# A two-layer-block transformer step on one core: the last mixer's recurrent chain in halves of the output partitions, and its value phase with the operands swapped

## The chip, the core and the metric

The program runs on one NeuronCore of a Trainium2 chip. Five engines matter: TensorE (PE, with its weight loads shown apart as PEld), VectorE (DVE), ScalarE (ACT), GpSimd (POOL) and the sync engine (SP), which issues most transfers. Each works its own queue in order. The metric is the device time of one execution in microseconds (us), lower is better; the figure compared is the median of several runs.

## The reference, cut to what matters

The whole computation is two blocks (`first_block`, `second_block`) over 256 tokens of width 1024. Only two parts of the second block are touched. The first is a gated delta-rule recurrence, run in two directions over 256 context tokens and then 256 tokens of x, with 16 heads of 64 channels:

```python
def wkv_scan(s0, scan_in):
    def step(s, inp):
        w, kk, a, k, v, r = inp
        sa = jnp.einsum('dbhij,dbhj->dbhi', s, kk)
        s = s * w[..., None, :] - sa[..., :, None] * (kk * a)[..., None, :] + v[..., :, None] * k[..., None, :]
        return s, jnp.einsum('dbhij,dbhj->dbhi', s, r)
    return lax.scan(step, s0, scan_in)
```

The second is the last layer of experts: each token has gates on 128 of 16384 experts, and the sum over experts is taken densely, expert row by expert row:

```python
        act = jax.nn.gelu(jnp.einsum('chkd,cd->chk', peer_u[eidx], xc))
        return jnp.einsum('chk,chkd->cd', (gate * act).astype(xc.dtype), peer_v[eidx])
```

## The kernel before

The last mixer is `layer2_mix`. Heads are taken two at a time, so a loop runs over eight pairs i. One round of it holds `chain(i)` (the recurrence of pair i), `inverse(i+1)` (`rw_inverse`, the triangular inverses that the next chain needs), `heads(i+1)` (`diff_head`, softmax attention), `scores(i+2)` (`rw_scores`, which makes the operands of a later chain) and some gate projections. The tile framework's scheduler orders the work of a round on each engine; an engine then runs its list strictly in that order. The last chain, i = 7, stands in `merge`, beside the branch projections (`br`).

`rw_chain` (L1710) cuts the 512 tokens into eight chunks of 64. In each chunk PE works in float32 (two records in the profile for one matmul; a transpose has one) through these steps, every one of which reads the one before:

- `vt` (L1728): two transposes turn 64 values of each direction; ACT copies them into the lower half of `UV` (L1729), whose upper half POOL sets to zero (L1725).
- `R`: state times `AL` (L1734, two matmuls of 128 columns, not in the first chunk), plus `MA` times `UV` over 128 rows, of which 64 are zero (L1738, four matmuls of 64 columns). All land on PSUM partitions 0 to 63. DVE copies the result (L1739).
- `U` (L1744): four matmuls with the inverse `TT`, 64 rows by 64 columns, again all on partitions 0 to 63 (the operands lie in the half that the pair's parity names). ACT negates and copies them into the upper half of `UV` (L1745).
- `Y`, in the last four chunks: `Y` from the state (L1749, two matmuls) and from `UV` (L1753, four matmuls, whose outputs alternate between partitions 0 to 63 and 64 to 127).
- `S` (L1760), in the first seven chunks: two matmuls of 128 columns that give the products of both heads with each other, of which half is then multiplied by the zeros of `WC`. DVE adds the old state (L1767) and multiplies by the decay `WC` (L1768).

`AL` is a copy, made by POOL (L1672), of `self.apart`, a single buffer in which one head stands beside zeros and into which both directions write in turn.

In `peer` the value phase (L2030 on) goes through 128 rows of `v`. A row is split into a high and a low float32r part, as are the gated activations `a`, and `mm` (L415) makes three matmuls of each product (L420 to L422). The row is the stationary operand: eight blocks of 128 columns, with the 256 tokens moving, so 24 matmuls of 256 columns to a row, into four PSUM accumulators laid out as output channels by tokens. Rows 48 to 111 of `a` come back from DRAM by loads on SP's queue (L2025).

## Time and profile before

| | us |
|---|---|
| median of three runs | 3560.41 (3560.06 to 3569.77) |
| the profiled execution | 3562.86 |
| its span in the profile | 3561.1 |
| the mixer's stage, 1520 to 2662 | 1142 |
| of that, the loop over pairs and its setup, to 2560 | 1040 |
| the value phase, first to last of its matmuls | 3139 to 3556 |

Over the span PE is busy 92%, DVE 64%, ACT 48% and POOL 21%. The busy time of PE is a model of pipelined matmuls, so two things are read beside it: when one group of matmuls starts and the next starts, which is the room that it takes in PE's list, and the waits printed behind a group, which name what PE stood still for. The granted clock of a stretch is a share of 2.4 GHz; 0.50 is 1.2 GHz.

### The profile page before, as it was taken

Reading aid. Unit: us, or ns where it says so; the run is one execution under the profiler, and the core shown is the slowest. Engines: PE = TensorE matmul, PEld = TensorE weight load, DVE = VectorE, ACT = ScalarE, POOL = GpSimd, SP = SyncE. Lnnn points to the kernel's source line nnn. Section 1 sums busy time; section 2 is a strip of 40 time slices with the busy share of each in tenths; the row PEclk is TensorE's granted clock in tenths of the full one; section 3 lists DMA queues with packets and bytes.
Section 4 is the critical chain, followed back from the end, with each engine's and each line's share of the span. In section 5 each row is a group of like instructions: output and inputs, shape, how many; then the busy total and the mean of one; then the engine's idle time right before and its main releaser. Section 6 shows DMA issues by size and latency. Waiting matters only on the chain.

```text
span 3561.1 us, 70098 instructions
## 1 busy us (share of the span) xinstructions
PE 3284.8 (92%) x27824; PEld 2789.4 (78%) x27824; DVE 2268.7 (64%) x4481; ACT 1707.5 (48%) x3116; POOL 732.7 (21%) x757
## 2 busy tenths in 40 slices
PE   6989889989999999977889999999889989999999
PEld 4869868866668888645677777767788989999999
DVE  3568847853359999546555655565447767756665
ACT  4445332442236666334334444444436657755554
POOL 0000322200000000013232323233308853300000
PEclk8999987899999999988878998899889999999999
DMA  7666573378788999951101111111336445555665
GB/s 292 243 222 228 208 248 111 122 296 349 320 364 326 341 333 336 379 184 49 32 29 38 52 44 38 35 47 53 115 116 206 163 140 177 174 193 190 232 213 166
DMA packets 164493, 658.65 MB, mean 185 GB/s; under 512 B 18216, under 2 KB 37304, under 8 KB 120256
## 3 DMA queue, kind: packets, MB, share of 16 engines
q1 hardware_dynamic: 149952, 580.72, 45.7%
q0 software_dynamic: 14208, 73.41, 5.7%
q8 instruction: 220, 3.60, 0.4%
q14 instruction: 113, 0.93, 0.1%
HBM read 634.26 MB, written 19.79 MB: 184 GB/s over the span
## 4 chain that ended last, share of the span: by engine, by line
PE 43%; DVE 8%; ACT 3%; issue 1%; DMA 1%; POOL 1%; SPq 0%; DVEq 0%; ACTq 0%; POOLq 0%
PE acc L421 3%; PE acc L420 3%; PE acc L422 3%; PE act L422 3%; PE act L421 3%; PE act L420 3%; PE G L1993 2%; DVE G L1808 1%; PE mc L1688 1%; PE U L1744 1%; PE R L1738 1%; DVE rs L366 1%; PE R L1734 1%; PE S L1760 1%; PE qk L420 1%
## 5 line engine op out<-in xcount | busy, mean ns | idle before, releaser
L1725 POOL MEMSET UV<- 64x256 f32 x64 | 19.4, 304 | 1007.0 <-DVE xT L1174 817.4
L427 PE MATMUL mg<-mg,xs 128*64 128x256 f32 x1408 | 184.9, 386 | 3.7 <-ACT xf L1100 3.7
L1247 ACT ACTIVATE msg<-mg 128x128 f32<-128x128 f32 (+1 forms) x154 | 42.1, 274 | 260.0 <-PE mg L427 190.7
L427 PEld LDWEIGHTS mg<-mg,xs 128*64 128x64 f32 x1408 | 106.1, 138 | 68.2 <-issue 15.8
L330 PE MATMUL mod<-wm,c 128*32 128x256 f32 x1152 | 99.7, 450 | 49.9 <-DMA wm<-mods 45.4
L327 POOL DMA_DIRECT2D wm<-mods x64 | 34.7, 543 | 389.0 <-PE mod L330 362.8
L330 PEld LDWEIGHTS mod<-wm,c 128*32 128x32 f32 x1152 | 37.5, 122 | 87.8 <-DMA wm<-mods 44.7
L1248 DVE TENSOR_TENSOR msg<-msg,mg 128x128 f32<-128x128 f32 (+1 forms) x154 | 43.3, 281 | 76.4 <-ACT msg L1247 75.9
L1983 POOL TENSOR_SCALAR oh<-iota,idx 128x128 f32<-128x128 f32 x44 | 58.3, 1324 | 146.4 <-PE G L1993 146.4
L366 DVE RECIPROCAL rs<-rs 128x256 f32<-128x256 f32 (+1 forms) x24 | 58.0, 2418 | 39.0 <-ACT rs L365 39.0
L1986 ACT ACTIVATE oh<-oh,idx 128x128 f32<-128x128 f32 x212 | 69.1, 393 | 6.9 <-DVE oh L1978 6.9
L1744 PE MATMUL U<-R,TT 64*64 64x64 f32 x512 | 49.4, 242 | 24.2 <-DVE R L1739 20.8
L1744 PEld LDWEIGHTS U<-R,TT 64*64 64x64 f32 x512 | 39.3, 149 | 41.0 <-DVE R L1739 24.2
L1745 ACT ACTIVATE UV<-U 64x256 f32<-64x256 f32 x64 | 24.0, 375 | 96.3 <-PE U L1744 96.1
L1978 DVE TENSOR_TENSOR oh<-iota,idx 128x1024 f32<-128x1024 f32 x53 | 67.6, 1278 | 0.0
L1993 PE MATMUL G<-oh 128*128 128x128 f32 x512 | 62.5, 275 | 0.0
L1151 DVE COPY mgt<-mg 128x128 f32<-128x128 f32 x44 | 12.8, 290 | 74.8 <-PE mg L1144 74.5
L1993 PEld LDWEIGHTS G<-oh 128*128 128x128 f32 x512 | 60.1, 192 | 0.0
L427 PE MATMUL ya<-md,mgt 128*64 128x512 f32 x176 | 55.1, 604 | 4.2 <-DVE mgt L1151 4.1
L1739 DVE COPY R<-R 64x256 f32<-64x256 f32 x64 | 26.5, 414 | 50.9 <-PE R L1738 50.5
L1767 DVE TENSOR_TENSOR S<-S,S 128x256 f32<-128x256 f32 x48 | 20.2, 421 | 56.7 <-PE S L1760 56.5
L1808 DVE TENSOR_TENSOR G<-G,X 128x1 f32<-128x1 f32 (+14 forms) x120 | 53.3, 444 | 3.6
(11876 smaller groups left out, 13541.5 us busy)
## 6 DMA issues: line engine op xcount, KB each, us to landing
mg<-m_gu SPq DMA_DIRECT2D x176, 1024.0 KB, 7.7
md<-m_dn SPq DMA_DIRECT2D x88, 1024.0 KB, 8.0
wm<-mods POOLq DMA_DIRECT2D x64, 1024.0 KB, 6.2
w<-u SPq DMA_DIRECT2D x128, 512.0 KB, 3.4
w<-v SPq DMA_DIRECT2D x128, 512.0 KB, 3.4
w<-w_in SPq DMA_DIRECT2D x132, 256.0 KB, 2.6
w<-e_gu SPq DMA_DIRECT2D x44, 512.0 KB, 4.2
w<-e_in SPq DMA_DIRECT2D x24, 512.0 KB, 4.3
```

The costliest lines, as they stand in the source:

```text
L330: nc.tensor.matmul(ps[32 * j:32 * j + 32, :256], c[:, 2 * kp + k, :], ws[:, 2 * j + k, :], start=kp + k == 0, stop=kp + k == 4)
L366: nc.vector.reciprocal(t[:, :n], t[:, :n])
L420: mm(ps, w.hi, h.hi, start=start, stop=False, **kw)
L421: mm(ps, w.hi, h.lo, start=False, stop=False, **kw)
L422: mm(ps, w.lo, h.hi, start=False, stop=stop, **kw)
L427: mm(ps, w, h, start=start, stop=stop, **kw)
L1744: nc.tensor.matmul(ps[:64, c0_:c0_ + 64], TT[hb, d, o, c], R[hb, d, o], start=True, stop=True)
L1808: v_.tensor_mul(pr[:, :t, :t], G[:, t:t + 1, :t].to_broadcast([128, t, t]), X[:, :t, :t].rearrange("p u s -> p s u"))
L1978: v_.tensor_tensor(o, iota.rearrange("p (a b i) -> p a b i", a=1, b=1).to_broadcast([128, 2, 4, 128]), idx[:, 0:2, 4 * t4:4 * t4 + 4].rear ...
L1983: nc.gpsimd.tensor_scalar(o[:, 0, t], iota, i1, w, op0=OP.is_equal, op1=OP.mult)
L1986: nc.scalar.activation(o[:, 0, t], o[:, 0, t], AF.Copy, scale=w)
L1993: nc.tensor.matmul(ps[:, 128 * t:128 * t + 128], o[:, 1, t], o[:, 0, t], start=True, stop=True)
```

## The change

**In the chain.** The two directions (for R and U) or the two heads (for S and Y) go to the two halves of the output partitions, in alternating matmuls of 64 columns. The state keeps only the products of a head with itself, as [128, 2, 64]; `WC` has no zeros. All values of a pair are turned before the first chunk by four transposes of 128 by 128, and `UV` is one tile for all eight chunks; nothing is set to zero. `MA` times `UV` reads the lower 64 rows alone and stands ahead of the state's part. ACT and DVE share the copy of U. S stands ahead of Y.

**Around it.** `AL` and `self.apart` are one set of four buffers, by parity and direction, so POOL's copies go. `rw_inverse` puts the directions on the two halves of the partitions and shares its copies between ACT and DVE. `lora` has one buffer for two, the gates' tile is shared with the squares of `rw_scores`, `diff_head` turns into a second buffer of `e1`, `merge` has one ring pair and one small tile less.

**In the value phase.** The activations are the stationary operand, in two blocks of 128 tokens, and half a row of `v`, 512 columns, moves: 12 matmuls a row. The spilled activations are loaded on POOL's queue, some rows ahead. At the end the four accumulators, now tokens by channels, are copied to SBUF and turned back by 16 transposes.

```diff
         for a in range(32):
-            nc.tensor.matmul(p2[:32, 16 * a:16 * a + 16], TT[half[0], a, 0:32], P1[half[0], a], start=True, stop=True)
+            d, e = divmod(a, 16)
+            nc.tensor.matmul(p2[32 * d:32 * d + 32, 16 * e:16 * e + 16], TT[half[d][0], e, 0:32], P1[half[d][0], e], start=True, stop=True)
...
+        UV = tp.tile([128, 8, 128], F32, tag="UV", name=f"UV{i}", bufs=UVB)
+        ps = self.psum("vt")
+        for j in range(4):
+            nc.tensor.transpose(ps[:, 128 * j:128 * j + 128], v[:, j // 2, 128 * (j % 2):128 * (j % 2) + 128], self.ident)
+        for h, e in enumerate((nc.scalar.copy, v_.tensor_copy)):
+            e(UV.rearrange("p (j h) x -> p h j x", h=2)[64:128, h], ps[dh[h]].rearrange("p (j x) -> p j x", j=4))
...
-            g_.memset(UV[0:64], 0.0)
...
+            for o in range(2):
+                for d in range(2):
+                    nc.tensor.matmul(ps[dh[d], 64 * o:64 * o + 64], MA[64:128, d, o, c], UV[64:128, js[d], dh[o]], start=o == 0, stop=c == 0 and o == 1, skip_group_check=True)
             if c:
+                for o in range(2):
+                    for d in range(2):
+                        nc.tensor.matmul(ps[dh[d], 64 * o:64 * o + 64], AL[d][:, c, o], S[:, d], start=False, stop=o == 1, skip_group_check=True)
+            v_.tensor_copy(R, ps[:, :128].rearrange("p (o x) -> p o x", o=2))
...
-            nc.scalar.activation(UV[0:64], ps[:64, :256].rearrange("p (d x) -> p d x", d=2), AF.Copy, scale=-1.0)
+            nc.scalar.activation(UV[0:64, js[0]], ps[dh[0], :128], AF.Copy, scale=-1.0)
+            v_.tensor_scalar(UV[0:64, js[1]], ps[dh[1], :128], -1.0, None, op0=OP.mult)
...
+                        nc.tensor.matmul(ps[dh[o], 64 * d:64 * d + 64], BKt[:, d, c, dh[o]], UV[:, js[d], dh[o]], start=True, stop=True)
...
-                    for m in range(KT):
-                        self.mm(acc[m // 2][:, T * (m % 2):T * (m % 2) + T], vs[:, m // 4, 128 * (m % 4):128 * (m % 4) + 128], a[:, j],
-                                i + j == 0 and m % 2 == 0, i + j == 127, skip_group_check=True)
+                    for hf in range(2):
+                        for t in range(2):
+                            self.mm(acc[2 * hf + t], a[:, j, 128 * t:128 * t + 128], vs[:, hf], i + j == 0, i + j == 127)
```

How the lists of the engines move is shown at three places. PE, one late chunk of a chain (the sixth of the last pair), before; R, U, Y, S are the PSUM tiles, the names behind the arrow the operands:

```order
L1734 MATMUL R_26323<-S_4_26313,AL_24886 64x128 x2
L1738 MATMUL R_26323<-UV_5_26316,MA_24887 64x64 x4
L1744 MATMUL U_26331<-R_5_26322,TT 64x64 x4
L1749 MATMUL Y_26337<-AL_24886,S_4_26313 128x64 x2
L1753 MATMUL Y_26337<-MR_24888,UV_5_26316 64x64 x4
L1760 MATMUL S_26345<-UV_5_26316,BKt_24889 128x128 x2
L1728 MATMUL vt_26353<-c_ident,v_25000 64x128 x2
```

And the same chunk in the changed kernel (the part with `AL` alternates twice between its two buffers; one turn is shown):

```order
L1733 MATMUL R_26344<-UV_26200,MA_24908 64x64 x4
L1737 MATMUL R_26344<-S_4_26330,AL_16721 64x64
L1737 MATMUL R_26344<-S_4_26330,AL_16722 64x64
...
L1742 MATMUL U_26354<-R_5_26343,TT_25511 64x64 x4
L1750 MATMUL S_26361<-UV_26200,BKt_24910 64x64 x4
L1763 MATMUL Y_26369<-AL_16721,S_4_26330 64x64 x2
L1763 MATMUL Y_26369<-AL_16722,S_4_26330 64x64 x2
L1766 MATMUL Y_26369<-MR_24909,UV_26200 64x64 x4
```

The transposes are gone from the chunk, the part of R that needs no state stands first, every matmul writes 64 by 64, and S has moved from behind Y to directly behind U.

DVE, a chunk in the middle of the loop (the fifth of a middle pair), before, from the copy of R; G, X are the triangular solve of `rw_inverse`, dst a softmax statistic:

```order
L1739 COPY R_4_21651<-R_21652 64x256
L1639 TENSOR_SCALAR kk_22482<-k_22400,c_pv 128x512
L1511 TENSOR_REDUCE dst_22335<-ds_22341 128x1
L1809 TENSOR_REDUCE X_21861<-G_21794 128x13
L1808 TENSOR_TENSOR G_21794<-G_21794,X_21861 128x14x14
```

And in the changed kernel, from the copy of R to the state's sum:

```order
L1738 COPY R_4_21652<-R_21653 128x128
L1807 TENSOR_REDUCE X_21870<-G_21803 128x14
L1545 SCALAR_TENSOR_TENSOR k_22416<-k_22417,c_pv,k_22416 128x2x255
L1806 TENSOR_TENSOR G_21803<-G_21803,X_21870 128x15x15
L1512 TENSOR_REDUCE dst_22353<-ds_22359 128x1
L1744 TENSOR_SCALAR UV_21545<-U_21663 64x128
L1546 SCALAR_TENSOR_TENSOR k_22416<-k_22417,c_pv,k_22416 128x2x255
L1807 TENSOR_REDUCE X_21870<-G_21803 128x15
L1757 TENSOR_TENSOR S_4_21675<-S_21670,S_3_21649 128x128
```

DVE has got a third step of the chain, the copy of one half of U (L1744 there), with other work queued ahead of it.

PE in the value phase, a piece of one row, before; acc are the accumulators, ap the split activations, w the split row:

```order
L420 MATMUL acc_33671<-ap50h,w28880h 128x256
L421 MATMUL acc_33671<-ap50l,w28880h 128x256
L422 MATMUL acc_33671<-ap50h,w28880l 128x256
L420 MATMUL acc_33672<-ap50h,w28880h 128x256
L421 MATMUL acc_33672<-ap50l,w28880h 128x256
L422 MATMUL acc_33672<-ap50h,w28880l 128x256
```

And in the changed kernel:

```order
L421 MATMUL acc_33699<-w28830h,ap100h 128x512
L421 MATMUL acc_33700<-w28830h,ap100h 128x512
L422 MATMUL acc_33699<-w28830l,ap100h 128x512
L423 MATMUL acc_33699<-w28830h,ap100l 128x512
L422 MATMUL acc_33700<-w28830l,ap100h 128x512
L423 MATMUL acc_33700<-w28830h,ap100l 128x512
```

Each matmul has 512 columns for 256, and there are half as many.

## Rows read from the trace of the kernel before

**Rows 1.** Stretches: us, busy and count of PE, PEld, DVE, ACT, POOL; clock; DMA

```profile
1520.00:2560.00 1040.00, 931.31 (x9406) 727.15 (x9403) 589.64 (x1096) 444.98 (x831) 307.04 (x342) 0.87 0.17 54
3145.00:3550.00 405.00, 405.00 (x3378) 405.00 (x3377) 253.26 (x381) 210.75 (x351) 0.00 (x0) 1.00 0.61 203
```

**Rows 2.** Groups, 1520 to 2662: PE records, busy us, mean ns, idle before

```profile
L1744 PE MATMUL U<-R,TT 64*64 64x64 f32 x512 | 49.4, 242 | 24.2 <-DVE R L1739 20.8 <-DVE TT L1866 3.1
L1738 PE MATMUL R<-UV,MA 128*64 128x64 f32 x512 | 47.7, 243 | 3.5 <-ACT UV L1729 3.5
L1760 PE MATMUL S<-UV,BKt 128*128 128x128 f32 x224 | 44.1, 326 | 6.1 <-ACT UV L1745 6.1
L1734 PE MATMUL R<-S,AL 128*64 128x128 f32 x224 | 41.3, 314 | 12.7 <-DVE S L1768 9.7 <-DVE S L1765 2.8
L1728 PE MATMUL vt<-c_ident,v 128*64 128x128 f32 x128 | 28.2, 304 | 0.7 <-ACT y L1754 0.3
L1749 PE MATMUL Y<-AL,S 128*128 128x64 f32 x128 | 24.4, 320 | 0.0
L1753 PE MATMUL Y<-MR,UV 128*64 128x64 f32 x256 | 17.5, 265 | 1.3 <-ACT UV L1745 1.0
```

**Rows 3.** Timeline, PE, one chunk with nothing beside it: start, us, records, idle before

```profile
2614.09 0.62 PE L1734 MATMUL R<-S,AL 128*64 128x128 f32 x4 [0.85 <-DVE S L1768]
2614.54 0.63 PE L1738 MATMUL R<-UV,MA 128*64 128x64 f32 x8
2615.68 0.67 PE L1744 MATMUL U<-R,TT 64*64 64x64 f32 x8 [0.51 <-DVE R L1739]
2616.29 0.66 PE L1749 MATMUL Y<-AL,S 128*128 128x64 f32 x4
2616.88 0.45 PE L1753 MATMUL Y<-MR,UV 128*64 128x64 f32 x8
2617.26 0.71 PE L1760 MATMUL S<-UV,BKt 128*128 128x128 f32 x4
2617.81 0.38 PE L1728 MATMUL vt<-c_ident,v 128*64 128x128 f32 x2
2619.04 0.51 PE L1734 MATMUL R<-S,AL 128*64 128x128 f32 x3 [0.85 <-DVE S L1768]
```

**Rows 4.** Timeline, PE, two groups of the last chunk, at 1.2 GHz

```profile
2627.33 1.11 PE L1744 MATMUL U<-R,TT 64*64 64x64 f32 x8 [0.51 <-DVE R L1739]
2629.41 0.70 PE L1753 MATMUL Y<-MR,UV 128*64 128x64 f32 x8
```

**Rows 5.** Timeline, DVE and ACT, the chunk of rows 3

```profile
2615.21 0.42 DVE L1739 COPY R<-R 64x256 f32<-64x256 f32 x1 [1.27 <-PE R L1738]
2616.45 0.38 ACT L1745 ACTIVATE UV<-U 64x256 f32<-64x256 f32 x1 [2.76 <-PE U L1744]
2617.38 0.27 ACT L1754 COPY y<-Y 128x128 f32<-128x128 f32 x1 [0.55 <-PE Y L1753]
...
2618.47 0.42 DVE L1768 TENSOR_TENSOR S<-S,WC 128x256 f32<-128x256 f32 x1
```

**Rows 6.** Timeline, PE, two steps of the inverse at 2.4 GHz

```profile
1716.05 2.20 PE L1844 MATMUL p<-T,MA 32*32 32x16 f32 x128
1722.85 2.19 PE L1848 MATMUL p<-P,TT 32*32 32x16 f32 x64
```

**Rows 7.** Timeline, DVE, an operation of `heads` with R's copy next in the list

```profile
2096.14 3.35 DVE L366 RECIPROCAL rs<-rs 128x512 f32<-128x512 f32 x1 [0.48 <-ACT rs L365]
```

**Rows 8.** Timeline, PE, first and ninth of nine float32r matmuls of 512 columns

```profile
2376.03 0.39 PE L420 MATMUL k<-h2h,w23210h 128*128 128x512 f32 x1
...
2377.85 0.39 PE L422 MATMUL k<-h2h,w23210l 128*128 128x512 f32 x1
```

**Rows 9.** Timeline, the end: last matmul, and the final multiplies on DVE

```profile
3555.74 0.28 PE L422 MATMUL acc<-ap126h,w29891l 128*128 128x256 f32 x1
3553.90 3.23 DVE L2042 SCALAR_TENSOR_TENSOR acts<-acc,mod,acts 128x256 f32<-128x256 f32 x8 [2.32 <-PE acc L422]
```

More of the change, by code (lines that the diff above doesn't have):

```diff
@@ L1573, in rwkv_setup @@
         self.pad = [p.tile([128, 16, 64], F32, name=f"pad{i}") for i in range(2)]
-        self.apart = xr[:, :1536].rearrange("p (c o t) -> p c o t", c=12, o=2)
-        for t in self.pad + [self.apart]:
+        ap = [[xr[:, :1536] if i + d == 0 else p.tile([128, 1536], F32, name=f"AL{i}{d}") for d in range(2)] for i in range(2)]
+        self.apart = [[t.rearrange("p (c o t) -> p c o t", c=12, o=2) for t in a] for a in ap]
+        for t in self.pad + ap[0] + ap[1]:
             nc.gpsimd.memset(t, 0.0)
@@ L1595, in rw_scores @@
         p, tp = self.rp, self.rt
-        lora = p.tile([128, 3, 128], F32, tag="lora", name=f"lora{i}", bufs=2)
+        lora = p.tile([128, 3, 128], F32, tag="lora", name=f"lora{i}", bufs=1)
         nc.sync.dma_start(lora, A["lora"][i])
@@ L1644, in rw_scores @@
         v_.tensor_mul(kk, kk, rs.rearrange("p (j t) -> p j t", j=2))
-        AL = p.tile([128, 2, 12, 64], F32, tag="AL", name=f"AL{i}", bufs=2)
+        AL = self.apart[i % 2]
         MA = p.tile([128, 2, 2, 8, 64], F32, tag="MA", name=f"MA{i}", bufs=2)
@@ L1723, in rw_chain @@
             s, cc = divmod(c, 4)
-            UV = tp.tile([128, 2, 128], F32, tag="UV", name="UV" + n)
-            g_.memset(UV[0:64], 0.0)
-            ps = self.psum("vt")
-            for d in range(2):
-                nc.tensor.transpose(ps[:64, 128 * d:128 * d + 128], v[:, s, 64 * (3 - cc if d else cc):64 * (3 - cc if d else cc) + 64], self.ident)
-            nc.scalar.copy(UV[64:128], ps[:64, :256].rearrange("p (d x) -> p d x", d=2))
-            R = tp.tile([128, 2, 2, 64], F32, tag="R", name="R" + n)
+            js = 4 * s + cc, 4 * s + 3 - cc
@@ L1745, in rw_chain @@
-            nc.scalar.activation(UV[0:64], ps[:64, :256].rearrange("p (d x) -> p d x", d=2), AF.Copy, scale=-1.0)
+                for o in range(2):
+                    for d in range(2):
+                        nc.tensor.matmul(ps[dh[d], 64 * o:64 * o + 64], AL[d][:, c, o], S[:, d], start=False, stop=o == 1, skip_group_check=True)
+            v_.tensor_copy(R, ps[:, :128].rearrange("p (o x) -> p o x", o=2))
+            ps = self.psum("U")
+            for o in range(2):
+                for d in range(2):
+                    nc.tensor.matmul(ps[dh[d], 64 * o:64 * o + 64], TT[dh[d], 8 * o + c], R[dh[d], o], start=True, stop=True)
@@ L1813, in rw_inverse @@
             nc.gpsimd.tensor_copy(self.pad[1][rr, :, 16 * b:16 * b + 16], X[rr].rearrange("p t s -> p s t"))
-        hb = 64 * (i % 2)
-        half = [slice(hb, hb + 32), slice(hb + 32, hb + 64)]
-        hb = slice(hb, hb + 64)
-        if i < 2:
-            self.TT = self.TT if i else p.tile([128, 32, 64], F32, name="TT")
-        TT = self.TT
-        Tv = TT[hb].rearrange("p i (b t) -> p t b i", b=4)
+        dh = [slice(0, 64), slice(64, 128)]
+        half = [[slice(64 * d + 32 * h, 64 * d + 32 * h + 32) for h in range(2)] for d in range(2)]
+        TT = p.tile([128, 16, 64], F32, tag="TT", name=f"TT{i}", bufs=2)
+        Tv = TT.rearrange("p i (b t) -> p t b i", b=4)
         for g in range(4):
@@ L1852, in rw_inverse @@
             for h in range(2):
-                nc.tensor.matmul(ps[32 * h:32 * h + 16, 16 * a:16 * a + 16], P1[half[h], a], TT[half[h], a, 32 * h + 16:32 * h + 32], start=True, stop=True)
-        for h in range(2):
-            nc.scalar.activation(TT[half[h], :, 32 * h + 16:32 * h + 32][0:16], ps[32 * h:32 * h + 16].rearrange("p (i t) -> p i t", i=32), AF.Copy, scale=-1.0)
+                d, e = divmod(a, 16)
+                o = 64 * d + 32 * h
+                nc.tensor.matmul(ps[o:o + 16, 16 * e:16 * e + 16], P1[half[d][h], e], TT[half[d][h], e, 32 * h + 16:32 * h + 32], start=True, stop=True)
+        for d in range(2):
+            for h in range(2):
+                o = 64 * d + 32 * h
+                pv = ps[o:o + 16, :256].rearrange("p (i t) -> p i t", i=16)
+                to = TT[half[d][h], :, 32 * h + 16:32 * h + 32][0:16]
+                if d:
+                    v_.tensor_scalar(to, pv, -1.0, None, op0=OP.mult)
+                else:
+                    nc.scalar.activation(to, pv, AF.Copy, scale=-1.0)
         for g in range(2):
@@ L2017, in peer, with load @@
             acc = [self.psum("acc") for _ in range(4)]
+            early = {}
+            def load(i):
+                if i < 128:
+                    early[i] = tp.tile([128, 2, T], F32, tag="a", name=f"a{i}", bufs=3)
+                    if i < HD:
+                        nc.gpsimd.dma_start(early[i], ad[(i - HF) // 2])
             def gated(i):
@@ L2029, in gated @@
                 return self.split(a, self.pair(tp, [128, 2, T], f"ap{i}", ("ah", "al")))
+            for i in range(HF, HF + 4, 2):
+                load(i)
             nxt = gated(0)
```

117 lines of the change are left out of this document (58 added, 59 removed).

## The prediction

> **What bounds the kernel now.** First the busy time by stretches. In the value phase PE is busy without a gap and the clock is full [rows 1]; every other engine is idle for a third of it or more, so the phase is as long as its matmuls. In the mixer's loop PE is busy 931 of 1040 us, at a granted clock of 0.87, and DVE, the next, 590 [rows 1]: PE is the bound there too, in 109 us of whose idle time it waits. Second the groups of the chain [rows 2]: their seven lines are busy 252.6 us between 1520 and 2662, and ahead of them stand waits of 24.2, 3.5, 6.1, 12.7, 0.7, 0 and 1.3 us, 48.5 us together. The largest wait is U's for DVE's copy of R, and DVE's list says why: it is in order, and a reciprocal of 3.35 us can stand in front [rows 7]. So both the chain's matmuls and the hops between them are on the path of this stage. Third a timeline of one chunk with nothing beside it [rows 3], where the room of a group is start to next start. The groups write one half of the output partitions, but for line 1753, whose matmuls alternate between the halves: it takes .38 us for eight records where U, of the same form 64 by 64, takes .61.
>
> I compare with the profiled execution, 3562.86 us with a span of 3561.1; the median of the runs is 2.4 us under it. Up to 1520 us both programs have the same lists.
>
> **The chain's matmuls.** Room per step at full clock [rows 3]: state part of R .45; UV part of R, eight records spaced (.63-.24)/7 = .056, so .45 (.24 is the mean of its records [rows 2]); U .61; state part of Y, four records spaced (.66-.32)/3 = .113, so .45; UV part of Y .38; S .55; vt two records of 128 columns at the same .113, so .22. A pair has 7, 8, 8, 4, 4, 7 and 8 of these: 3.15 + 3.6 + 4.88 + 1.8 + 1.52 + 3.85 + 1.76 = 20.56 us. Afterwards 38 steps (8 for the UV part of R, 8 U, 7 state parts, 7 S, 4 and 4 for Y) have the form of line 1753, four matmuls of 64 columns in alternating halves: 38 x .38 = 14.44. The four large transposes take 4 x .113 = .45. That is 14.89, a gain of 5.67 a pair and 45.4 for eight.
>
> That is at 2.4 GHz. At 1.2 GHz U and line 1753 take 1.11 and .70 [rows 4], .41 apart, where by the same reckoning (record's start to last end) they are .67 - .45 = .22 apart at full clock [rows 3]: 1.86 times as much. A mean clock of .87 [rows 1] is 26% of the time at the lower level, in which some 15% of the work is done, so the gain grows by 1 + .15 x .86 = 1.13: **-51.3 us**. Bounds: the busy sums of [rows 2] give 252.6 against 38/32 of line 1753's 17.5 x 8 = 166 and 5 for the transposes, so -81; and if only U, the state part of Y and S come down, the steps that are least like it, 8 x (8 x .23 + 4 x .07 + 7 x .17) x 1.13 = -30.
>
> For this price the two halves must run side by side in one PSUM tile also where they read different rows of the array, as U and the state part of Y will. Two steps of the inverse say that they do: 128 records that read two halves of the rows take 2.20 us, 64 that read one half take 2.19 [rows 6], a second half for nothing. The Trainium skill (TensorEngine Tiling (Array Packing), Gotcha 1: PSUM Pressure) says that different row tiles cannot access the same PSUM bank simultaneously, which is against this change; the trace does not agree with it, and the rival below says what it would give.
>
> **The hops.** The wait of R for ACT's copy of vt goes: **-3.5** [rows 2]. R's copy and the two steps of the state handle half as many elements in a partition; 128 by 128 takes .27 on ACT where 128 elements more take .42 on DVE [rows 5]. Most of that is hidden in the loop, where PE has other work; I take **-2**. The new hop is DVE's copy of one half of U, which stands in the order behind the solve and other work. The nearest row is U's own wait for DVE, 20.8, of 64 hops [rows 2]; it replaces the waits for ACT, 6.1 + 1.0, so **+13.7**, with bounds of 0 (DVE is done with it by the time ACT is) and +20.8.
>
> Four chunks of the last pair have nothing beside them. Their cycle is 2619.04 - 2614.09 = 4.95 us [rows 3]. After it I put, for one turn: state part of R .38 and .2 for the tail of its last record (.63 - .45 for R [rows 3]), copy .27, U .38 and .2, copy .27, S .38 and .2, two DVE operations of .27 each; with six handovers of .04 to .10 (R's last record ends at 2615.17, the copy starts at 2615.21 [rows 3, 5]) that is some 3.2, as the UV part of R and Y lie under DVE's part. The gain is 1.75 a chunk, of which (5.67 - .45 - .88)/8 = .54 to .83, for a chunk with Y, is counted above: 4 x .92 = **-3.7**.
>
> **What is costed at nothing.** POOL's copies into `AL` and its zeros: POOL is busy 307 of 1040 [rows 1] and no wait of [rows 2] names it; if it did matter, it could only be a gain. The inverse's halves: the number and the size of its matmuls stay; the copies that DVE gets and those that it gives to ACT are about even. ACT, 445 of 1040 busy [rows 1], has room for the further switches of its function that the halves bring. `lora` with one buffer: SP waits until the last reader of the pair before is done, and the loads of weights queued behind it wait too; no wait of [rows 2] is for a transfer, so the cover is the lead of those loads, and if it were gone each pair would pay a load. The gates' tile shared with the squares: ACT waits for the gates' write to DRAM, with softmax and U's copies queued behind it; cover is ACT's idle half, price if it is gone some 1 us in 16 places. One ring pair less in `merge`: its projections are fed from a ring that still has eight, and PE there waits for the chain.
>
> **The value phase.** Before, 3072 matmuls at 405/3378 = .1199 us [rows 1]: 368.3. After, 1536 of 512 columns. Nine of that form and type earlier in the program start (2377.85 - 2376.03)/8 = .2275 apart [rows 8]; I take .2285, for the turn from one row to the next: 351.0. The difference is **-17.3**, with bounds of -10 (.2335, as the activations are loaded anew for each) and -19. What hides the rest: DVE 253 and ACT 211 of 405 [rows 1] split the rows, which come 4.5% faster; DMA at 0.61 has the same room. The loads of spilled activations change from SP's queue, behind the rows of `v`, to POOL's, which has nothing to do [rows 1], and are issued earlier; SP's list only loses them.
>
> At the end, the last matmul starts at 3555.74, and of eight multiplies DVE had begun the first at 3553.90, since accumulators were done one after another; they take .40 each [rows 9]. After it, all wait for the last rounds: two copies of 128 by 512 (at .27 for 128 elements, some .8), transposes under the multiplies, 8 x .40: the end moves from 2.7 to 5.7 us behind the last matmul, before the transfer: **+3**, bounds 0 and +5.
>
> **Sum.** -51.3 - 3.5 - 2 + 13.7 - 3.7 - 17.3 + 3 = -61.1. The span comes to 3500 and the profiled execution to some 3502, the median to **3500** us.
>
> **The rivals.** *The waits take over*: the steps get shorter, yet PE finds nothing to put in their place and stands for DVE instead; for it speaks that U already waits 20.8 us for DVE and that DVE gets more of the chain, against it that 590 of 1040 leaves room [rows 1, 2]. If half of the 51.3 comes back as waits, 3526; chance .18. *The waits shrink as well*: with fewer steps of other engines in a turn, no transposes and a part of R ahead of the state, half of the 48.5 us goes [rows 2] and the new hop costs nothing, 3500 - 13.7 - 24 + 6 (counted already) = 3468; chance .17. *Rows of the array do not run side by side into one bank*: U and the state part of Y stay at .61 and .45 [rows 3], 8 x (8 x .23 + 4 x .07) x 1.13 = 19 us, 3519. [Rows 6] speak against it; chance .05. The rule named above would be this. *Slower: the clock*. In this stage PE's clock falls to 1.2 GHz after waits, and its mean is .87 [rows 1]. The changed stage leaves PE less work: 1040 x .87 = 905 us at full clock, 854 without 51. If its gaps make the clock fall more often, work and time are tied by 854/clock: .81 makes 1054, which uses up both gains of the chain and the value phase's; from there on it is slower, and .78 gives 1095, 55 more than before, and with the value phase's 14 off that is 3601. Against it: the wait of U, the longest, is not a new one. Chance .06. *It does not do what it says*, that is, the halves alternate in the order but the engine takes them one by one as before: rows 3 show line 1753 doing it, so .02 at most, with the value phase alone left, 3545.
>
> **How the numbers follow.** The forecast, .52; waits take over .18; waits shrink .17; rows of the array .05; clock .06; nothing in the chain .02. The range of 3450 to 3540 holds the first four but for the far ends, some .8; it takes in the -81 for the matmuls (3470) together with smaller waits, and the -30 together with +20.8 for the hop (3528). A measurement of this kernel tells some 0.3%, 10.7 us, from no change. Faster by more than that, under 3549.7: the first four, .92; within: .03, the last case, which lies 5 us from that bound, and the near part of the clock's; slower: .05.
>
> **What will show it.** U, both parts of R, S and the first part of Y at line 1753's price: some .38 us start to start in the bare chunks of the last pair, and their busy sum near 170 in place of 252.6. U's wait for DVE about as before, and a wait of S and of the UV part of Y for DVE's half of U of some 20 us, where ACT's 7 stood. Cycles of 3.2 us in the last chunks. A clock of .85 or more in the stretch to 2500. Accumulating matmuls .2285 us apart. The end 5 to 6 us behind the last of them. It would be wrong if waits for DVE in the chain come to 70 us, if U has kept .61 us, or if the clock falls under .82.

## The result

The changed kernel takes **3527.11 us** (median of 4 runs, 3523.05 to 3530.41) where the kernel before takes 3561.36 (4 runs, 3560.06 to 3569.77): ratio 0.9894, 95% interval 0.9876 to 0.9913. That is 34 us less by the medians. 60 were forecast, and 3527 lies inside the range of 3450 to 3540. The profiled execution has a span of 3521.0 us, 40.1 less than before.

Where the 40.1 us come from, by the starts of the same matmuls in both traces:

| | before | after | difference |
|---|---|---|---|
| mixer's stage, 1520 us to the last matmul of `res` | to 2672.7 | to 2643.8 | -28.9 |
| from there to the first accumulating matmul | 466.6 | 467.6 | +1.0 |
| accumulating matmuls, first to last start | 416.4 | 400.5 | -15.9 |
| from the last one's start to the end | 5.3 | 9.1 | +3.8 |

### The profile page after: what moved, and what is told of

It is laid out like the page before. It is cut to its first block, busy times and chain, and to the rows that moved or that the text cites. A ratio compares the mean times of both kernels' runs of the same rounds, so it can differ in the third digit from the quotient of the medians.

```text
span 3521.0 us, 67859 instructions
## 1 busy us (share of the span) xinstructions
PE 3223.7 (92%) x26784; PEld 2655.6 (75%) x26784; DVE 2295.1 (65%) x4603; ACT 1697.7 (48%) x3077; POOL 711.2 (20%) x688
## 3 DMA queue, kind: packets, MB, share of 16 engines
q8 instruction: 212, 3.47, 0.4%
## 4 chain that ended last, share of the span: by engine, by line
PE 41%; DVE 7%; ACT 3%; issue 2%; DMA 2%; POOL 1%; SPq 0%; ACTq 0%; POOLq 0%; DVEq 0%
PE act L423 3%; PE act L422 3%; PE act L421 3%; PE acc L422 3%; PE acc L421 3%; PE acc L423 3%; PE G L2002 2%; DVE G L1806 1%; PE mc L1686 1%; PE mc L1679 1%; ACT L363 1%; PE v L422 1%; PE qk L421 1%; PE v L421 1%; PE qk L422 1%
## 5 line engine op out<-in xcount | busy, mean ns | idle before, releaser
L428 PEld LDWEIGHTS mg<-mg,xs 128*64 128x64 f32 x1408 | 105.1, 137 | 67.5 <-issue 16.1
L2035 POOL DMA_DIRECT2D a<-ad x32 | 17.3, 542 | 285.5 <-DVE ap48l L446 127.1
L1743 ACT ACTIVATE UV<-U 64x128 f32<-64x128 f32 x64 | 17.3, 270 | 76.3 <-PE U L1742 76.1
L428 PE MATMUL yb<-md,mgt 128*64 128x512 f32 x176 | 54.0, 592 | 0.0
L1742 PE MATMUL U<-R,TT 64*64 64x64 f32 x512 | 35.5, 255 | 20.1 <-DVE R L1738 10.5
L2007 ACT COPY Gate<-G 128x288 f32<-128x288 f32 x64 | 43.3, 678 | 20.4 <-DVE acts L2006 20.4
```

Of the source, the lines that this page charges most:

```text
L428: mm(ps, w, h, start=start, stop=stop, **kw)
```

## The profile after

The chain's groups in the changed kernel (PE, 1520 to 2644 us; records, busy us, mean ns, and the waits ahead of them), to be held against [rows 2]:

```profile
L1742 PE MATMUL U<-R,TT 64*64 64x64 f32 x512 | 35.5, 255 | 20.1 <-DVE R L1738 10.5 <-DVE TT L1875 8.6 <-ACT T L1833 0.9
L1750 PE MATMUL S<-UV,BKt 128*64 128x64 f32 x448 | 33.8, 255 | 9.5 <-DVE UV L1744 5.4 <-ACT UV L1743 4.1
L1733 PE MATMUL R<-UV,MA 64*64 64x64 f32 x512 | 33.3, 248 | 5.6 <-DVE S L1757 5.1 <-DVE UV L1722 0.4
L1737 PE MATMUL R<-S,AL 128*64 128x64 f32 x336 | 27.6, 251 | 5.1 <-DVE S L1755 3.5 <-DVE S L1758 1.3
L1766 PE MATMUL Y<-MR,UV 128*64 128x64 f32 x256 | 18.8, 268 | 3.9 <-DVE UV L1744 2.4 <-ACT UV L1743 1.3
L1763 PE MATMUL Y<-AL,S 64*64 64x64 f32 x192 | 13.9, 259 | 0.0
L1737 PE MATMUL R<-S,xT 128*64 128x64 f32 x112 | 13.2, 244 | 2.6 <-DVE S L1758 2.6
L1763 PE MATMUL Y<-xT,S 64*64 64x64 f32 x64 | 5.6, 255 | 0.0
L1720 PE MATMUL vt<-c_ident,v 128*128 128x128 f32 x32 | 5.5, 295 | 1.2 <-DVE v L1546 1.2
```

(`xT` is the first of the four `AL` buffers, which lies in an older tile.) The busy sum is 187.2 us, 252.6 before; the waits are 48.0, 48.5 before. The matmuls became cheaper and the chain's waits stayed. What rose stands in other groups. The same view, first before (1520 to 2672.7 us), one group of the scores (`mc`) and two of the inverse:

```profile
L1681 PE MATMUL mc<-xT,BK 128*128 128x128 f32 x128 | 24.2, 349 | 1.4 <-DVE BK L1677 1.4
L1825 PE MATMUL tb<-c_ident,pad 128*64 128x128 f32 x128 | 24.4, 318 | 16.0 <-DVE pad L1812 12.0 <-DVE TT L1827 2.9 <-ACT TT L1827 1.1
L1861 PE MATMUL p<-P,MA 32*32 32x32 f32 x512 | 21.1, 197 | 1.6 <-DVE TT L1866 1.4 <-ACT TT L1855 0.2
```

And after, where the group of the scores is printed in two, by the buffer it reads:

```profile
L1679 PE MATMUL mc<-AL,BK 128*128 128x128 f32 x96 | 21.1, 386 | 5.7 <-DVE BK L1675 5.7
L1679 PE MATMUL mc<-xT,BK 128*128 128x128 f32 x32 | 7.4, 397 | 7.8 <-DVE BK L1675 7.8
...
L1821 PE MATMUL tb<-c_ident,pad 128*64 128x128 f32 x128 | 21.4, 290 | 13.8 <-DVE TT L1823 8.8 <-DVE pad L1810 5.0
L1870 PE MATMUL p<-P,MA 32*32 32x32 f32 x512 | 21.7, 200 | 7.6 <-DVE TT L1862 3.1 <-DVE TT L1875 2.9 <-ACT UV L1722 1.6
```

The stage as one stretch (us, busy us and count of PE, PEld, DVE, ACT, POOL; granted clock; DMA), before and after:

```profile
1520.00:2672.70 1152.70, 1028.31 (x10179) 817.91 (x10176) 638.40 (x1199) 485.86 (x911) 328.08 (x374) 0.87 0.19 62
```

```profile
1520.00:2643.80 1123.80, 984.25 (x10662) 762.80 (x10658) 660.38 (x1319) 470.90 (x868) 288.56 (x273) 0.86 0.21 63
```

For more than that I summed over PE's records: a group's **room** (start to next start, less the wait), its waits, and the time at 1.2 GHz by the trace's record of the granted clock. The chain's room fell from 216.3 to 147.5 us, the rest of the stage's, the same work, rose from 811.8 to 836.7; waits outside the chain rose from 76.0 to 91.6; the time at 1.2 GHz from 294 us in 29 pieces to 311 in 38. All of the scores' waits went from 1.4 to 14.5 us and the inverse's from 19.2 to 25.6. In the two views of the stage DVE is busy 22 us more, ACT 15 and POOL 40 less.

The bare chunks of the last pair show the clock best (timeline, PE, DVE and ACT; start, us, idle before), to be held against [rows 3]:

```profile
2582.10 0.45 PE L1737 MATMUL R<-S,AL 128*64 128x64 f32 x8 [1.27 <-DVE S L1758]
2582.95 0.69 PE L1742 MATMUL U<-R,TT 64*64 64x64 f32 x8 [0.39 <-DVE R L1738]
2583.68 0.27 ACT L1743 ACTIVATE UV<-U 64x128 f32<-64x128 f32 x1 [2.56 <-PE U L1742]
2583.99 0.29 DVE L1744 TENSOR_SCALAR UV<-U 64x128 f32<-64x128 f32 x1 [1.09 <-ACT UV L1743]
2584.01 0.81 PE L1750 MATMUL S<-UV,BKt 128*64 128x64 f32 x8 [0.37 <-ACT UV L1743]
...
2584.74 0.69 PE L1763 MATMUL Y<-AL,S 64*64 64x64 f32 x8
...
2585.37 0.69 PE L1766 MATMUL Y<-MR,UV 128*64 128x64 f32 x8
2585.99 0.69 PE L1733 MATMUL R<-UV,MA 64*64 64x64 f32 x8
...
2586.61 0.69 PE L1737 MATMUL R<-S,AL 128*64 128x64 f32 x8
...
2587.79 0.69 PE L1742 MATMUL U<-R,TT 64*64 64x64 f32 x8 [0.49 <-DVE R L1738]
```

A step takes .62 us start to start and a cycle 2587.79 - 2582.95 = 4.84: all four chunks run at 1.2 GHz, where the first two before ran at 2.4. The granted clock fell at 2582.65, .3 us ahead of the first U shown and behind the wait of 1.27 us. DVE's half of U waits for ACT's half.

The end (timeline, last matmuls, copies, transposes, multiplies), to be held against [rows 9]:

```profile
3508.53 0.39 PE L422 MATMUL acc<-w29321l,ap126h 128*128 128x512 f32 x1
3508.75 0.39 PE L423 MATMUL acc<-w29321h,ap126l 128*128 128x512 f32 x1
3508.98 0.39 PE L422 MATMUL acc<-w29321l,ap126h 128*128 128x512 f32 x1
...
3511.93 0.40 PE L423 MATMUL acc<-w29331h,ap126l 128*128 128x512 f32 x1
3512.16 0.60 PE L2072 MATMUL yT<-c_ident,acts 128*128 128x128 f32 x4
3512.36 0.69 DVE L2065 COPY acts<-acc 128x512 f32<-128x512 f32 x1 [0.68 <-PE acc L423]
3512.97 1.88 DVE L2073 SCALAR_TENSOR_TENSOR acts<-yT,mod,acts 128x256 f32<-128x256 f32 x4
```

## The experiments

Each edit is made in the changed kernel, unless said otherwise. The kernel before took 3564 to 3567 us on the chips of these runs; ratios are against it. The changed kernel itself stands at .9894 (.9876 to .9913), measured where the kernel before took 3561, and was not run again on those chips. Single executions of one kernel lie up to 32 us apart (3524 to 3556 for the mixer alone), so a difference in one trace says less than one between medians whose intervals part.

**The parts apart.** First the kernel before with the new value phase (lines 2018 on replaced).

> The kernel before, with the new value phase alone (activations stationary, 512 columns of v moving, spilled activations on POOL's queue, turn at the end). Theory: the two parts of the change add up, so this is worth what the two traces differ by behind the gate phase: matmuls first to last 416.4 before, 400.5 after, -15.9, and the end 3.7 longer, so -12 and a time near 3549; the mixer's stage stays at 1142 us. Rival, the value phase gained only because the mixer left the clock or the queues in another state: a difference from -12 by more than 4 us.

3554.16 us, ratio .9972 (.9951 to .9993): -10, where 12 was expected. Its trace has 398.5 us from first to last accumulating matmul, 416.4 before.

Then the changed kernel with the old value phase.

> The changed kernel with the value phase of the kernel before, so the change of the mixer alone. Theory, the two parts add up: 3527 plus 12, some 3539, with the mixer's stage ending near 2644 us. Rival, the value phase takes something from what stands ahead of it (the loads on POOL's queue, the place of buffers): a difference from 12 by more than 5.

3537.90 us, ratio .9935 (.9903 to .9967). The two shortfalls, .28% and .65%, make .93%, and the whole change has 1.06%: the parts add up within the intervals. The value phase came as forecast; the question is the mixer's.

**Is it the alternation that makes a step short?**

```diff
-            for o in range(2):
-                for d in range(2):
+            for d in range(2):
+                for o in range(2):
                     nc.tensor.matmul(ps[dh[d], 64 * o:64 * o + 64], TT[dh[d], 8 * o + c], R[dh[d], o], start=True, stop=True)
```

and likewise in R, S and Y.

> The changed kernel, with the matmuls of R, U, S and Y in the other order, so that both of one half of the output partitions stand together and then both of the other; same count, same sizes. Theory, it is the alternation that makes a step short: U, the UV part of R and the state part of Y go back to some .61 us, the others to .45, 8 x .23 + 8 x .23 + 4 x .23 + 7 x .07 x 2 + 4 x .07 = 5.9 us a pair at full clock, 47 for eight and 53 with the slow stretches; of the chain's 69 us less room the stage kept 29, so of these 53 some 22 would show, 3549. Rival, the steps are short because each matmul writes 64 columns and the engine overlaps neighbours in any order: within 5 us of the changed kernel, and U's room unchanged at some .060 us a record.

3516.93 us, ratio .9865 (.984 to .989): no slower. My theory fell, and on the step the rival is right: U stays short. PE's timeline of a bare chunk:

```profile
2573.70 0.45 PE L1763 MATMUL Y<-AL,S 64*64 64x64 f32 x8
2574.09 0.46 PE L1766 MATMUL Y<-MR,UV 128*64 128x64 f32 x8
2574.48 0.46 PE L1733 MATMUL R<-UV,MA 64*64 64x64 f32 x8
2574.86 0.46 PE L1737 MATMUL R<-S,AL 128*64 128x64 f32 x8
```

A step is .39 us with the halves one after the other and .38 in turn (median over all undisturbed U at full clock: .385 and .378). Before, all four matmuls of U went to one half, and it was .605. What counts is that the four go to two halves of the output at all: the UV part of R in the changed kernel, whose operands all lie in one half of the rows, takes .378 too. The eight records of a U start in four close pairs in either order (7 ns apart in turn, 13 one after the other), where before they came one by one, 58 ns apart.

**Does DVE's copy of half a U cost what I said?**

```diff
             nc.scalar.activation(UV[0:64, js[0]], ps[dh[0], :128], AF.Copy, scale=-1.0)
-            v_.tensor_scalar(UV[0:64, js[1]], ps[dh[1], :128], -1.0, None, op0=OP.mult)
+            nc.scalar.activation(UV[0:64, js[1]], ps[dh[1], :128], AF.Copy, scale=-1.0)
```

> The changed kernel, with both halves of U copied by ACT, one after the other, so that the chain has one hop to DVE less. Theory, the prediction's term for the new hop (+13.7): S and Y stop waiting for DVE (7.8 us in the trace), and the time falls by 5 to 10, to some 3519. Rival, the hop costs nothing, since DVE's half only followed ACT's anyway: within 3 us of 3527.

3532.66 us (3519.21 to 3551.20), ratio .9917 (.9883 to .995). No gain was measured. The edit puts a second ACT copy in place of the hop and gives another order, so it doesn't price the hop by itself. The chain's waits did fall, from 47.9 to 37.9 us in its trace, but those elsewhere rose from 91.6 to 105.1.

**DVE's half waits for ACT's half.** In the trace of the changed kernel all 64 of these copies wait for a semaphore that ACT raises, with two PSUM tiles 7 of 64.

```diff
-            ps = self.psum("U")
+            pu = [self.psum("U"), self.psum("U")]
...
-                    nc.tensor.matmul(ps[dh[d], 64 * o:64 * o + 64], TT[dh[d], 8 * o + c], R[dh[d], o], start=True, stop=True)
-            nc.scalar.activation(UV[0:64, js[0]], ps[dh[0], :128], AF.Copy, scale=-1.0)
-            v_.tensor_scalar(UV[0:64, js[1]], ps[dh[1], :128], -1.0, None, op0=OP.mult)
+                    nc.tensor.matmul(pu[d][dh[d], 64 * o:64 * o + 64], TT[dh[d], 8 * o + c], R[dh[d], o], start=True, stop=True)
+            nc.scalar.activation(UV[0:64, js[0]], pu[0][dh[0], :128], AF.Copy, scale=-1.0)
+            v_.tensor_scalar(UV[0:64, js[1]], pu[1][dh[1], :128], -1.0, None, op0=OP.mult)
```

> The changed kernel, with the two halves of U in two PSUM tiles. In the changed kernel DVE's copy of its half waits for ACT's copy of the other in each of 64 chunks (42.5 us of DVE's idle time), though both only read. Theory, they wait since they share a PSUM tile: DVE's copy starts with ACT's, and S waits .3 us less in each bare chunk; cycles there go from 4.84 to some 4.6 us, the waits of S and Y for the halves of UV from 13.4 to some 9, and the time by 3 to 6 us, to 3522. Rival, in the loop it is DVE's queue and not ACT that keeps the half: DVE's wait goes and the time stays within 3 us.

3497.90 us (3492.21 to 3499.58), ratio .9811 (.9787 to .9835): 29 us under the changed kernel, five times what I had put. The copies do run side by side now, and the bare chunks start at full clock. Its timeline of one:

```profile
2555.84 0.45 PE L1742 MATMUL U<-R,TT 64*64 64x64 f32 x8 [0.39 <-DVE R L1738]
2556.32 0.27 ACT L1743 ACTIVATE UV<-U 64x128 f32<-64x128 f32 x1 [2.36 <-PE U L1742]
2556.37 0.29 DVE L1744 TENSOR_SCALAR UV<-U 64x128 f32<-64x128 f32 x1 [0.58 <-PE U L1742]
2556.64 0.45 PE L1750 MATMUL S<-UV,BKt 128*64 128x64 f32 x8 [0.35 <-ACT UV L1743]
...
2559.10 0.45 PE L1742 MATMUL U<-R,TT 64*64 64x64 f32 x8 [0.48 <-DVE R L1738]
```

The cycle is 3.26 us, the 3.2 of the prediction. But 29 us is more than the copies can give: S waits .02 us less in a chunk. Two kernels test that: two tiles with both copies on ACT, so that nothing runs side by side, and two tiles without alternation. Their diffs are those above, together.

> The kernel with the two halves of U in two PSUM tiles, and both of them copied by ACT, one after the other. Theory A, the two tiles gained 29 us because the two copies now run side by side: here they don't, and the time is that of the kernel with one tile and both copies on ACT, 3533, within 10. Theory B, the gain was from the other turn of the two PSUM banks: 3498 within 10, as with the two tiles and both engines. Theory C, the time of such variants scatters by 10 to 15 us, since each gives another order and another pattern of the clock: somewhere between, and U, S and R with the waits of either.

3503.67 us, ratio .9832 (.9796 to .9868): the gain is there without the copies side by side, 29 us against one tile with both on ACT. Theory A falls.

> Both edits together: two PSUM tiles for U, and the matmuls in the order without alternation. The latter alone was worth -10 us although it made each step 6 ns longer, so it shifts little but the clock and the order. If the gain of the two tiles is one of their own, this kernel is within 10 us of 3498; if it was the luck of one order, it falls back towards 3517 to 3527.

3496.14 us, ratio .9798 (.9769 to .9827), 21 us under its like with one tile. Two tiles gained in each of three pairs, and not by what they were made for. (A fourth pair, with additional matmuls in the last pair of heads, comes below: 3523 against 3504, with intervals that overlap.) What the tiles did change is the order that the scheduler lays out, as is shown below for all kernels.

**S ahead of Y** was a part of the change that I had not priced. Undone, by moving the block of S behind that of Y:

> The changed kernel, with S behind Y again as in the kernel before. In a bare chunk DVE's two steps on the state then begin .76 us later at full clock and 1.25 at 1.2 GHz, with the UV part of R (.38 or .62) in between, so a cycle grows by .4 to 1.0 us, or the clock rises as PE's waits change their place: 0 to +4 for the last pair. In the loop other work covers it: no change but the scatter of another order, which the kernels so far put at 10 us. Altogether 3527 to 3535, unless that scatter is larger than thought.

3499.69 us, ratio .9824 (.9789 to .986): 27 us faster than with S ahead. In PE's bare chunk one sees a part of it:

```profile
2563.54 0.45 PE L1742 MATMUL U<-R,TT 64*64 64x64 f32 x8 [0.39 <-DVE R L1738]
2563.82 0.40 PE L1750 MATMUL Y<-AL,S 64*64 64x64 f32 x8
2564.36 0.66 PE L1753 MATMUL Y<-MR,UV 128*64 128x64 f32 x8
2564.85 0.40 PE L1759 MATMUL S<-UV,BKt 128*64 128x64 f32 x8
...
2566.82 0.45 PE L1742 MATMUL U<-R,TT 64*64 64x64 f32 x8 [0.39 <-DVE R L1738]
```

The first part of Y needs no U and fills the hop in which S ahead waits .36 us. One wait of PE is printed in a cycle, not two, and all four chunks stay at 2.4 GHz with no work added: 3.28 us a cycle against 4.84, 6 us for the four. The place of S is not the only difference: here PE has projections right up to the R of the first bare chunk, where the changed kernel waits 1.27 us.

**Is it too little work that lets the clock fall?**

```diff
+            if i == KT - 1 and c > 3:
+                fill(S)
             v_.tensor_copy(R, ps[:, :128].rearrange("p (o x) -> p o x", o=2))
...
+            if i == KT - 1 and c > 3:
+                fill(R)
             nc.scalar.activation(UV[0:64, js[0]], ps[dh[0], :128], AF.Copy, scale=-1.0)
```

`fill(x)` is one matmul of x with itself, 128 by 128 by 128, into a tile of its own.

> The changed kernel, with one additional matmul of 128 by 128 by 128, whose result nobody reads, behind R and one behind U in the last four chunks of the last pair, where PE has nothing else to do in those two hops (.36 to .49 us idle, the matmul takes .23 at full clock). Theory, the four chunks run at 1.2 GHz (4.84 us a cycle) because PE has too little to do there since the change: with more work for it the clock stays up, a cycle takes some 3.3 us, and the tail gains up to 6 us, 3521. Rival, it is the waits themselves or what came before that set the level: the clock falls at the same place and the cycle is 4.84 or, with the additional matmul in the way, up to 5.2: 3527 to 3529.

3523.17 us, ratio .9886 (.9854 to .9917), by itself no measurable difference from .9894; the last pair shows it. PE's timeline:

```profile
2580.54 0.45 PE L1741 MATMUL R<-S,AL 128*64 128x64 f32 x8 [0.82 <-DVE S L1767]
...
2581.48 0.45 PE L1749 MATMUL U<-R,TT 64*64 64x64 f32 x8
2581.86 0.49 PE L1726 MATMUL F<-R 128*128 128x128 f32 x2
...
2584.40 0.49 PE L1726 MATMUL F<-S 128*128 128x128 f32 x2
2584.86 0.45 PE L1749 MATMUL U<-R,TT 64*64 64x64 f32 x8
```

Between the last five U there are 4.35, 3.38, 3.39 and 3.39 us, with more work on PE, where there were 4.72, 4.85, 4.84 and 4.84. (The first of the four lies ahead of the bare chunks, at full clock in both.) The clock stays up. The stage ends 5.9 us earlier. That fits the theory, but doesn't single it out: the additional matmuls also fill the waits, and the wait ahead of the first bare U is .82 us here and 1.27 there. And the kernel without alternation, with waits of .36 and .49 us in a chunk and nothing added, ran the first two of its three bare cycles at full clock (3.65 and 3.64 us), two tiles without alternation its only two (3.47 and 3.42).

With two tiles it had less to add:

> Both edits that helped together: two PSUM tiles for U, and the additional matmuls in the bare chunks of the last pair. In the kernel with two tiles the first two bare chunks already run at full clock (3.26 and 3.23 us a cycle) and the third falls to 4.45, so the additional matmuls have only some 1 to 2 us left to gain there: 3495 to 3498. If the gain of the two tiles were one order's luck, which this edit of the last pair leaves as it is, the loop comes out as before and the sum is the same; if the clock's pattern in the loop differs from run to run it scatters by 10.

3504.37 us (3493.46 to 3519.27), ratio .985 (.9806 to .9894): the bare chunks all run at full clock (3.58 a cycle, with the additional matmuls), and the total is no better than without. The spread over runs of one kernel covers it.

Then the same in every chunk of every pair, with two tiles:

> Two PSUM tiles for U, and the two additional matmuls in every chunk of every pair: 120 of them, 27.6 us of PE at full clock. Theory, the stage loses some 140 us to its half clock (280 us at 1.2 GHz), which follows PE's waits (131 us); work that fills waits keeps the clock up, so the time grows by less than the 27 us or not at all, and the stretch at 1.2 GHz shrinks by 20 us or more. Rival, in the loop the additional matmuls don't fall into the waits, since the order gives other work the place and the waits come from late engines: plus 25 to 35 us, 3523 to 3533, and the waits of PE stay at 131.

3545.41 us, ratio .9945 (.9925 to .9964): 47 us slower. The rival is right and more. The chain's waits did fall, from 43.8 to 23.5 us, but its room rose by 46 and the time at 1.2 GHz from 280 to 314. In the loop this additional work did not hold the clock. Nor did the clock fall after waits alone: of its 29 falls in the trace of the kernel before, 20 have 1 us or more of PE's waits in the 5 us ahead of them, but 6 have .11 us at most, with PE on the inverse's matmuls of 32 rows and 16 or 32 columns.

**The inverse's shared copies**, put back on one engine each:

```diff
-            for d, e in enumerate((nc.scalar.copy, v_.tensor_copy)):
+            e = nc.scalar.copy if g % 2 else v_.tensor_copy
+            for d in range(2):
                 e(Tv[dh[d], 4 * g:4 * g + 4], ps[:64].rearrange("p (t b i) -> p t b i", t=4, b=4)[:, :, :, 16 * d:16 * d + 16])
...
-        v_.tensor_scalar(P1[dh[1]], pv[:, 16:], od[:64], None, op0=OP.mult)
+        nc.scalar.activation(P1[dh[1]], pv[:, 16:], AF.Copy, scale=od[:64])
...
-                if d:
-                    v_.tensor_scalar(to, pv, -1.0, None, op0=OP.mult)
-                else:
-                    nc.scalar.activation(to, pv, AF.Copy, scale=-1.0)
+                nc.scalar.activation(to, pv, AF.Copy, scale=-1.0)
```

> The changed kernel, with the copies of the inverse that the change shares between ACT and DVE put back on one engine each (the two halves of a transposed block both on ACT or both on DVE in turn, the two others on ACT). Theory, sharing costs there too, since DVE's half waits for ACT's half in the same PSUM tile: the inverse's waits on PE go from 25.6 back to some 19 (before: 19.2), and the time by -5 or so. Rival, the sharing shortens the inverse as it was meant to: without it the waits grow and the time is 3 to 10 longer.

3528.12 us, ratio .9888 (.9849 to .9928): the same. The inverse's waits do go back, from 25.6 to 17.3 us, but the time does not follow; other groups take the waits.

**All of them side by side**, from one profiled execution each (sums over PE's records, 1520 us to the last matmul of `res`):

| kernel | ratio | stage ends | waits of PE | at 1.2 GHz | room outside the chain |
|---|---|---|---|---|---|
| before | 1 | 2672.7 | 124 | 294 | 812 |
| value phase only | .9972 | 2667.8 | 121 | 297 | 810 |
| changed | .9894 | 2643.8 | 140 | 311 | 837 |
| mixer only | .9935 | 2651.7 | 138 | 317 | 847 |
| inverse one engine | .9888 | 2647.9 | 138 | 307 | 840 |
| U on ACT | .9917 | 2655.4 | 143 | 341 | 846 |
| fill in the last pair | .9886 | 2637.9 | 137 | 294 | 834 |
| no alternation | .9865 | 2630.1 | 127 | 290 | 828 |
| two tiles | .9811 | 2614.6 | 131 | 280 | 818 |
| two tiles, ACT | .9832 | 2625.5 | 131 | 290 | 828 |
| two tiles, no alternation | .9798 | 2625.5 | 128 | 273 | 826 |
| two tiles, fill in the last pair | .985 | 2620.4 | 127 | 294 | 824 |
| S behind Y | .9824 | 2619.1 | 130 | 294 | 831 |
| two tiles, fill everywhere | .9945 | 2668.2 | 114 | 314 | 843 |

Among the eleven kernels from "changed" to "S behind Y" two groups show: waits of 137 us and more with a stage that ends at 2638 to 2655, and waits of 127 to 131 with 2615 to 2630. Between them lie some 10 us of waits and, by the means of 314 and 287, 27 us at 1.2 GHz, which cost half of that: together 24 us, and the means of the ends, 2647.3 and 2622.5, are 25 apart. So the account closes. It is no law: the kernel with fill everywhere has the fewest waits, 114 us, and 314 us at 1.2 GHz. And the scatter is large beside it: the changed and the mixer-only kernel, whose mixer is the same code, end 8 us apart, as do the nearest members of the two groups. By the medians and their intervals two tiles (alone, with ACT, without alternation) and S behind Y are faster than the changed kernel; the kernel without alternation and the one with two tiles and fill are not clear of it.

That the order differs can be read from the traces. PE's list of groups in the stage (one group is a run of matmuls into one PSUM tile, the additional ones left out) is all but the same in the changed kernel, mixer only and fill in the last pair: 99.8% of it stands in the same sequence, and 99.9% for two tiles and two tiles with fill in the last pair. Each of the other small edits leaves only 40% to 72% of the changed kernel's list in sequence. So such an edit replaces the stage's whole order. Which difference in the order costs the 10 us of waits, and what comes first, the waits or the lower clock, stays open.

One cost is not of the order: the scores' waits, 1.4 us before, are 9.9 to 15.0 in all twelve kernels of the table that have the new mixer. No run undid what the change did around the scores (the shared buffers of `AL`, the work moved from POOL and ACT to DVE), so its cause is not shown.

## Why the prediction was right or wrong

| term | forecast | measured |
|---|---|---|
| matmuls of the chain (room) | -51.3 | -68.8 |
| hops: -3.5, -2, +13.7 (waits of the chain) | +8.2 | -0.5 |
| bare chunks beyond that | -3.7 | within the two above |
| room of the stage's other work | 0 | +24.9 |
| waits of the stage's other work | 0 | +15.6 |
| between mixer and value phase | 0 | +1.0 |
| value phase, matmuls | -17.3 | -15.9 |
| value phase, end | +3 | +3.8 |
| sum | -61.1 | -39.9 (spans: -40.1) |

**The price of a step was right, its gain too low.** .38 us was forecast for all steps, and .378 to .382 is what they take at full clock. The 45.4 at full clock was too little: by the records the chain fell from 182.0 to 124.2 us of work at full clock, 57.8. The steps before were priced too low (20.56 x 8 = 164.5 against 182.0), by a slip in the reading: the UV part of R, the state part of Y and vt were taken by the spacing of their records (.45, .45, .22), which leaves out the time from the last record to the next group, while U and line 1753 were taken from start to next start, which has it. From start to next start they take .558, .588 and .310 (medians at full clock); for the state part of Y [rows 3] say so, 2616.29 to 2616.88. With these, and .488 for the state part of R, the eight pairs come to 183. The cycle of 3.2 us for the bare chunks is met at full clock (3.26 with two tiles); in the changed kernel it is 4.84, at 1.2 GHz, so the term of -3.7 was priced at the wrong clock.

**Rows of the array in one PSUM bank.** The rival at 3519 is out. U, whose two halves read different rows, takes .378 us with both in one tile and .379 with two tiles. The Trainium skill (TensorEngine Tiling (Array Packing), Gotcha 1: PSUM Pressure) says that different row tiles cannot access the same PSUM bank simultaneously; these runs show no cost of it.

**The new hop was mis-sized.** +13.7 was the price of U's queueing behind DVE, and the chain's waits did not rise at all: S and the UV part of Y wait 13.4 us for the halves of U, 7.8 of them for DVE's, where some 20 were expected. In 23 of the 64 chunks DVE stood idle until ACT's half was done (42.5 us); in the others DVE was at other work until then, or nearly. With both copies on ACT nothing was gained.

**The step that failed is the sum's silence on the rest of the stage,** which it put at nothing. I took the 26% of the time at 1.2 GHz as given, and only let it multiply the gain. But PE was left with less work and as many hops. The time at 1.2 GHz rose by 17 us while the stage shrank by 29, the other work took 24.9 us more room, and other groups' waits grew by 15.6. (The kernel with the new value phase alone, whose mixer is the old one, has 297 us at 1.2 GHz and 810 of room, so these steps are larger than the scatter between two traces of one mixer.) Of the 24.9, 9.9 are there at full clock too (726.1 to 736.0), so some 15 are the clock. The rival "the waits take over" named this time, 3526, but not the place: the waits are the scores' for DVE's `BK` (12.1 us more) and the inverse's for DVE's `TT`, not the chain's. I had called the copies that DVE gets and gives about even, and DVE is busy 22 us more in the stage; that this makes the scores wait is likely but was not tested. The clock rival had part of the mechanism, at far too high a price. Of "costed at nothing", the inverse's halves did cost waits (6.4 us more, back when undone), though no time. `lora` in one buffer, the shared gates' tile, the second `e1` and the buffers of `AL` were not undone in any run, so what they cost or gave is open. No wait in the chain's groups names a transfer.

**S ahead of Y** I had taken for a gain that needs no price, since DVE's steps on the state get the cover of Y. In the bare chunk it makes no cycle shorter (3.26 with S ahead, in two tiles, and 3.28 behind, both at 2.4 GHz) and takes the work out of the hop from U to S.

**The value phase** went as costed: matmuls .227 us apart, -15.9 against -17.3; the end 9.1 us behind the last start where 5.3 were. (The last multiply ended 1.4 us behind the last matmul's start before, by [rows 9], and not 2.7, and ends 5.0 behind it now; the difference was near the forecast.)

So the forecast of 3500 is what kernels with the same matmuls give in a better order: 3496 to 3504 for five of them (one with eight matmuls more). That number is in part luck: in the trace with two tiles the chain's matmuls gave 71.8 us of room where 51.3 were forecast, and the stage's other work took 18.4 more, in room and waits, where nothing was. Why the order of the changed kernel is worse is open. Two tiles together with S behind Y were not run.

## What to carry to other kernels

Price a shorter step by a row of the same form, but ask then what the engine does in the time that it is given back: where it waits for hops that did not shrink, the clock can fall and take a part of the gain, also from work that nobody touched (some 15 us here). Look in a dependent chain for work that fits the hop before moving what looks urgent ahead of it. And where a scheduler lays out the whole stage anew, two or three harmless variants tell how much of a difference is the order and not the edit; here that was 25 to 30 us, as much as the change in the mixer itself.

## What the runs showed of the hardware that I had not expected

- Four float32 matmuls of 64 by 64 took .605 us on one half of the output partitions and .378 on two (start to next start at 2.4 GHz), and it hardly mattered (.385) whether the halves alternate or come one after the other.
- In the changed kernel the bare chunks, in which PE stands for .36 and for .49 us, ran at 1.2 GHz, all four, and with one more matmul of 128 columns in each of these gaps at 2.4 GHz, all four: the cycle fell from 4.84 to 3.39 us by adding work. The same gaps with nothing added also ran at 2.4 GHz, for two cycles of 3.65, in the kernel without alternation.
- The same addition in every chunk of the loop made the kernel 47 us slower, at 314 us of the lower clock in place of 280.
- Of the 29 falls of the clock in the stage before, 6 came with .11 us of waits at most in the 5 us ahead, while PE ran the inverse's matmuls of 32 rows.
